# A hybrid decoder layer on one core: where two weight blocks are rounded, which engine makes their low halves, and where the skip factors are scaled

## The chip, the cores and the metric

The kernel runs on one core of one Trainium2 chip. The metric is the device time of one execution, in microseconds (us). Shorter is better. The engines are TensorE (PE: matmuls, with PEld for its weight loads), VectorE (DVE), ScalarE (ACT), GpSimd (POOL) and SyncE (SP, which here only issues DMA transfers). Each engine takes its instructions in the order of its own program.

## The reference, cut to what matters

One layer with 512 tokens of 1024 channels: a normalization, one wide projection, three causal token mixers whose results are gated and added, and a feed-forward part.

```python
h = rms_norm(x, norm1_g[l])
u = h @ w_in[l]                      # 512 x 1024 times 1024 x 11512
(dq, dk, dv, iq, ik, iw, nq, nkv, ng, sz, sxbc, sdt, mg) = jnp.split(u, offsets, axis=-1)
y_a = dsa_mixer(...); y_b = nsa_mixer(...); y_c = ssd_mixer(...)
...
y = y_diag + y_off + xs * d_skip     # in ssd_mixer: d_skip are the skip factors, one for each of 32 heads
...
x = x + mix @ w_out[l]
x = x + jnp.square(jax.nn.relu(rms_norm(x, norm2_g[l]) @ w_ff1[l])) @ w_ff2[l]
```

## The kernel before, in words

**Matmuls in halves.** Every operand of a projection is held as a rounded high half and a low half (the operand minus its high half). `mm3` issues three matmuls for each product: high by high, high by low, low by high. For the activations these halves are `hTh` and `hTl`, for the weights `whi` and `wlo`.

**The start.** x comes in four tiles of 128 tokens (t = 0 to 3). A tile is scaled, turned by eight TensorE transposes into two PSUM buffers `pT` (four transposes each), copied by ScalarE into `hTh` (line 431) and subtracted by VectorE into `hTl` (line 432), once for each half of the tile. There are two `pT` buffers, so the transposes of a tile wait until the `hTl` of the tile before has read them.

**The weight stream.** The class `WS` holds a list of weight blocks of up to 128 x 1024 elements. `load` brings a block into one of three raw buffers (`wraw`) through SP's queue. `split` rounds it on ScalarE (`whi`, line 170) and subtracts on GpSimd or VectorE (`wlo`, line 172); there are six buffers of each half. The set `LOWP` names the blocks whose low half GpSimd makes: block 0 and blocks 4 to 23. Blocks 0 to 3 are the first projection, `c0` (456 columns: keys, values, index parts). Blocks 4 to 11 are the second, `nkv`: 4 to 7 have 512 columns, 8 to 11 have 304. A raw buffer comes free when `wlo` of its block is done.

**The first projection.** `c0` runs tile by tile into two PSUM buffers `pj`. Tiles 0 and 1 fill them; tile 2 can start when the copies of tile 0 (`u0`, lines 682 and 683, and `v_d`, lines 544 and 545) have read its buffer.

**What sets the order.** The program is written as two coroutines, the mixers (`main`) and the projections (`filler`), that take turns by estimated costs. A scheduler then fixes the order on each engine before the run, by priorities and by its own estimate of the times. `tc.issue_after(x)` makes an instruction come after the instruction x in that plan. A small change in one place can so alter the order of many later ones.

**The mixers.** After the start comes the DSA mixer (scores over selected keys), then the state scan of the SSD mixer (16 steps of one group and one chunk, `ssd`, from about 395 us to 556 us), then the NSA mixer, the gated branches and the feed-forward part; projections fill TensorE between the mixers' matmuls. In a scan step, DMA loads `xz` (two buffers), GpSimd makes `xt` and `xw` from it and multiplies it by the skip factors `dskip` (line 1277), and TensorE multiplies `xt` by the decay matrix `E` (line 1303). `ssd_prelude2`, a part of the work between the DSA mixer's units, makes the scan's factors, among them `sv_ea`, and halves `dskip` (line 1226).

Of the kernel before, what the change touches and what calls it, by code (L numbers as in the profile page):

```python
# [9 lines left out]
AF = mybir.ActivationFunctionType  # L10
ALU = mybir.AluOpType
# [12 lines left out]
NS = 6  # L24
RAWB = 3
LEAD = 3
LOWP = {0} | set(range(4, 24))
WE = 2
NH = 4
BH = 2  # L30
# [3 lines left out]
PSB = {"pj": 2, "sc": 2, "pT": 2, "pv": 1, "pF": 1}  # L34
HM = 4000
HP = 3000
WARM = 4, 2
R0, R1, R2, R3 = 1000.0, 1.5, 2.5, 0.5


def build_kernel(ctx, tc, A, out):
    nc = tc.nc
    pe, act, dve, pool = nc.tensor, nc.scalar, nc.vector, nc.gpsimd
# [5 lines left out]
    def bc(ap, shape):  # L49
        return ap.to_broadcast(shape)  # L50

    def f(ap):
        return ap.bitcast(F32)
# [36 lines left out]
    def ps(tag, shape, dt=F32, bufs=2):  # L90
        if tag == XT[0]:
            XT[1] += 1
            if XT[1] % 3 == 0:
                tag = "pF"
        return psp.tile(shape, dt, tag=tag, name=tag, bufs=PSB[tag])
# [9 lines left out]
    hTh = hp_.tile([128, KT, S], F32R, name="hTh")  # L105
    hTl = hp_.tile([128, KT, S], F32R, name="hTl")
# [16 lines left out]
    p = ps("pF", [128, 512])  # L123
# [8 lines left out]
    class WS:  # L132
# [24 lines left out]
        def split(s):  # L157
            i = s.nsplit
            while s.nload <= i:
                s.load()  # L160
            _, n, w = s.specs[i]
            r = s.raw.pop(i)
            m = n * w
            after = None
            if callable(r):
                after = r.after
                r = r(False)
            hi = wp.tile([128, 1024], F32R, name="whi", tag="whi", bufs=NS)
            lo = wp.tile([128, 1024], F32R, name="wlo", tag="wlo", bufs=NS)
            act.activation(hi[:, :m], r[:, :m], AF.Copy)  # L170
            with tc.issue_after(H0[0][1]) if i == 1 else nullcontext():
                (pool if i in LOWP else dve).tensor_tensor(lo[:, :m], r[:, :m], f(hi[:, :m]), op=ALU.subtract)  # L172
            s.hl[i] = (hi[:, :m].rearrange("p (a b) -> p a b", b=w), lo[:, :m].rearrange("p (a b) -> p a b", b=w))
            s.nsplit += 1
            if after is not None:
                after()
# [105 lines left out]
    for q in range(3):  # L282
        m = 0
# [32 lines left out]
    dskip = cp.tile([128, 32], F32, name="dskip")  # L316
# [51 lines left out]
    ss1 = cp.tile([128, NB], F32, name="ss1")  # L368
    rs1 = cp.tile([128, NB], F32, name="rs1")
    H0, XG, g1p = [], [], []  # L370
    wm = ps("pv", [128, 512])

    def warm(n, ref=None):
        with tc.issue_after(getattr(ref, "ins", ref)) if ref is not None else nullcontext():
            for _ in range(n):
                pe.matmul(wm[:, 0:128], ident, ident, start=True, stop=True)
    with tc.high_priority(offset=2 * HP):
        warm(WARM[0])
    ones = x0.tile([128, 128], F32, name="ones")
# [3 lines left out]
    for t in range(NB):  # L383
        with tc.high_priority(offset=0 if t else HP):
            if t == 1:
                with tc.issue_after(H0[0][0]):
                    act.activation(sq_junk, xt[t], AF.Square, accum_out=ss1[:, t:t + 1])
            elif t:
                act.activation(sq_junk, xt[t], AF.Square, accum_out=ss1[:, t:t + 1])
            else:  # L390
                act.activation(sq_junk[:, 0:512], xt[0][:, 0:512], AF.Square, accum_out=ssh[:, 0:1])
                dve.tensor_tensor_reduce(xg, xt[0][:, 512:], xt[0][:, 512:], 1.0, 0.0, ALU.mult, ALU.add, accum_out=ssh[:, 1:2])
                dve.tensor_tensor(ss1[:, 0:1], ssh[:, 0:1], ssh[:, 1:2], op=ALU.add)
                for k0 in range(0, KT, 4):
                    p = ps("pT", [128, 4, 128])
                    for k in range(4):
                        i_ = pe.transpose(p[:, k], xt[t][:, (k0 + k) * 128:(k0 + k + 1) * 128], ident)
                    xg_ = x0.tile([128, 4, 128], F32, name=f"xg{k0}")
                    dve.tensor_tensor(xg_, p, bc(g1c[:, k0:k0 + 4, None], [128, 4, 128]), op=ALU.mult)
                    XG.append(xg_)  # L400
                warm(WARM[1], i_)
            dve.tensor_scalar(ss1[:, t:t + 1], ss1[:, t:t + 1], 1.0 / D, EPS, op0=ALU.mult, op1=ALU.add)
            pool.tensor_tensor(rs1[:, t:t + 1], ss1[:, t:t + 1], mhalf[:, :1], op=ALU.pow)
            if t:
                for i, c in enumerate((0, 512)):
                    dve.scalar_tensor_tensor(xt[t][:, c:c + 512], xt[t][:, c:c + 512], rs1[:, t:t + 1], g1p[i], op0=ALU.mult, op1=ALU.mult)
            else:
                dg = x0.tile([128, 128], F32, name="dg")
                dve.tensor_scalar(dg, ident, rs1[:, 0:1], None, op0=ALU.mult)
                rb = ps("pF", [128, 512])[:, 0:128]  # L410
                i_ = pe.matmul(rb, ones, dg, start=True, stop=True)
                for c in (0, 512):
                    p = ps("sc", [128, 512])
                    with tc.issue_after(getattr(i_, "ins", i_)):
                        pe.matmul(p, one1, g1w[:, c:c + 512], start=True, stop=True)
                    g1p.append(p)
            for k0 in range(0, KT, 4):
                if t:
                    p = ps("pT", [128, 4, 128])
                    for k in range(4):  # L420
                        pe.transpose(p[:, k], xt[t][:, (k0 + k) * 128:(k0 + k + 1) * 128], ident)
                else:
                    hsl = (slice(None), slice(k0, k0 + 4), slice(0, 128))
                    xg_ = XG[k0 // 4]
                    dve.tensor_tensor(xg_, xg_, bc(rb[:, None, :], [128, 4, 128]), op=ALU.mult)
                    h0 = act.activation(hTh[hsl], xg_, AF.Copy)
                    l0 = dve.tensor_tensor(hTl[hsl], xg_, f(hTh[hsl]), op=ALU.subtract)  # L427
                    H0.append([getattr(i, "ins", i) for i in (h0, l0)])
                    continue
                hsl = (slice(None), slice(k0, k0 + 4), slice(t * 128, t * 128 + 128))  # L430
                act.activation(hTh[hsl], p, AF.Copy)
                dve.tensor_tensor(hTl[hsl], p, f(hTh[hsl]), op=ALU.subtract)

    caus = tri("caus", 512, NEG, 0.0, 384, 1, -1)
    vism = tri("vism", 128, NEG, 0.0, -31, 1, 0, [[128, 4], [-16, 32]]).rearrange("p (b n) -> p b n", b=4)
# [2 lines left out]
    for i, b in enumerate((2, 3)):  # L438
        for half in range(2):
            cur = 2 * b + half  # L440
            r = slice(64 * half, 64 * half + 64)
# [770 lines left out]
    def ssd_prelude2(sv, t, tri1, dta):  # L1212
        ones = t["u"]
        pool.memset(ones, 1.0)
        p = ps("pT", [128, 512])
        pe.matmul(p[:, 0:128], tri1, dta, start=True, stop=True)
        pe.matmul(p[:, 128:256], ones, dta, start=True, stop=True)
        dve.tensor_copy(sv["acm"], p[:, 0:128])
        dve.tensor_scalar(sv["nac"], p[:, 0:128], -1.0, None, op0=ALU.mult)
        act.activation(sv["dec"], p[:, 128:256], AF.Exp)  # L1220
        dve.tensor_tensor(t["b"], p[:, 128:256], sv["acm"], op=ALU.subtract)
        act.activation(sv["dw"], t["b"], AF.Exp)
        dve.scalar_tensor_tensor(sv["dw"], sv["dw"], 2.0, sv["dth"], op0=ALU.mult, op1=ALU.mult)
        act.activation(sv["ea"], sv["acm"], AF.Exp)
        dve.tensor_scalar(sv["ea"], sv["ea"], 0.5, None, op0=ALU.mult)
        dve.tensor_scalar(dskip, dskip, 0.5, None, op0=ALU.mult)
        yield 700.0

    def ssd_prelude3(sv, t):
# [438 lines left out]
    def main():  # L1668
        nonlocal at
        HI[0] = 0  # L1670
        yield from dsa_index(mk)
        yield "dq"
        yield "nkv"
        sv, *rest = yield from ssd_prelude()
        at = popen("att", side="right")
        HI[0] = HM
        us = dsa_units()
        us[5].load = lambda: ssd_prelude2(sv, *rest)
        us[7].load = lambda: ssd_prelude3(sv, rest[0])
        yield from pipeline(us, R1)  # L1680
        pclose("att")
        pclose("pre")
        pclose("mask")
        yield from ssd(sv, R3)
        XT[0] = "pT"
        yield "nq"
        at = popen("att", side="right")
        yield from pipeline(nsa_units(R2), R2)
        done.add("nsa")
        yield "c1"  # L1690
        pclose("att")
        pclose("kv")
# [5 lines left out]
    def step():  # L1698
        try:
            v = next(fg)  # L1700
        except StopIteration:
            alive[0] = False
            return None
        return v
# [3 lines left out]
    while True:  # L1708
        with tc.high_priority(offset=HI[0]):
            r = next(mg, None)  # L1710
# [6 lines left out]
        else:  # L1717
            debt += r
            while debt > 0 and alive[0]:
                v = step()  # L1720
# [32 lines left out]
```

## Time and profile before

| what | us |
|---|---|
| median of three timed runs | 1395.9 |
| their range | 1394.72 to 1400.18 |
| the profiled execution, its own time | 1403.27 |
| span of its trace | 1401.5 |
| TensorE busy in that span | 1369.0 |
| VectorE busy | 1001.1 |
| ScalarE busy | 722.0 |
| GpSimd busy | 286.8 |

The profiled execution's own time is 1.8 us above the span of its trace, and 7.4 us above the median of the timed runs, so differences are read from the trace and set on the median. Over the span TensorE was granted 0.986 of its full clock.

### The profile page before, as it was taken

The numbers are of one execution on the slowest core, as the hardware profiler recorded it, in microseconds if no ns is written. First come the engines' busy times: TensorE is split into PE (matmuls) and PEld (weight loads), VectorE is DVE, ScalarE is ACT, GpSimd is POOL, SyncE is SP. The second block draws the span as 40 slices with busy tenths as digits, with TensorE's granted clock in tenths as the row PEclk, the third lists the DMA queues.
The fourth block names the chain that finished last, engine by engine and source line by source line (L and its number), as shares of the span: only waits on it lengthen the run. The fifth ranks groups of instructions, "written<-read, shape, count | busy, mean of one in ns | idle before, by whom it ended". The sixth has DMA issues, their size and how long they took to land.

```text
span 1401.5 us, 19674 instructions
## 1 busy us (share of the span) xinstructions
PE 1369.0 (98%) x6875; PEld 1142.1 (81%) x6875; DVE 1001.1 (71%) x1962; ACT 722.0 (52%) x1434; POOL 286.8 (20%) x235
## 2 busy tenths in 40 slices
PE   8989999999999999999999999999899999999998
PEld 7878888888877778888887888788789888888887
DVE  6499977999877656477667788888635575767841
ACT  5545436667666756366565566555224444444430
POOL 3445211111047375100000002133100201102000
PEclk9999999999999999999999999999999999999999
DMA  6335654644486687735435453435444665746531
GB/s 192 89 96 144 166 179 132 166 113 123 121 259 223 190 257 201 188 100 140 114 114 157 118 146 111 122 117 177 143 150 140 118 177 127 174 116 132 157 117 52
DMA packets 222721, 205.35 MB, mean 147 GB/s; under 512 B 15497, under 2 KB 170013, under 8 KB 222622
## 3 DMA queue, kind: packets, MB, share of 16 engines
q1 hardware_dynamic: 206652, 180.49, 43.7%
q0 software_dynamic: 15232, 20.98, 8.2%
q10 hardware_dynamic: 738, 2.63, 0.6%
q8 instruction: 54, 0.88, 0.3%
q14 instruction: 45, 0.37, 0.1%
HBM read 167.56 MB, written 36.51 MB: 146 GB/s over the span
## 4 chain that ended last, share of the span: by engine, by line
PE 77%; DVE 7%; DMA 7%; issue 4%; POOL 3%; ACT 2%; SPq 0%; DVEq 0%; POOLq 0%; ACTq 0%
PE pj L451 18%; PE pj L453 18%; PE pj L452 18%; PE sc L451 3%; PE sc L452 3%; PE sc L453 3%; DMA gld<-g_d 3%; PE pT L931 2%; PE sc L893 2%; PE sc L892 2%; PE pv L944 2%; DMA wraw<-in_w_in_dram 1%; PE pv L943 1%; POOL mixf L1488 1%; PE sc L1303 1%
## 5 line engine op out<-in xcount | busy, mean ns | idle before, releaser
L170 ACT ACTIVATE whi<-wraw 128x1024 fp32r<-128x1024 f32 (+2 forms) x190 | 198.3, 1048 | 233.8 <-PE pj L452 115.7
L172 DVE TENSOR_TENSOR wlo<-wraw,whi 128x1024 fp32r<-128x1024 f32 (+1 forms) x169 | 215.7, 1280 | 104.5 <-ACT whi L170 102.9
L451 PE MATMUL pj<-hTh,whi 128*128 128x512 f32 x384 | 153.6, 400 | 0.2 <-DVE cacc L824 0.2
L453 PE MATMUL pj<-hTh,wlo 128*128 128x512 f32 x384 | 152.6, 397 | 0.0
L452 PE MATMUL pj<-hTl,whi 128*128 128x512 f32 x384 | 152.3, 397 | 0.0
L451 PE MATMUL pj<-whi,hTh 128*128 128x512 f32 (+2 forms) x352 | 138.7, 394 | 5.9 <-DVE stk L521 3.2
L901 ACT ACTIVATE p<-p,nb,rs 128x256 f32<-128x256 f32 (+3 forms) x192 | 123.2, 645 | 30.6 <-DVE nb L899 30.6
L453 PE MATMUL pj<-whi,hTl 128*128 128x512 f32 (+2 forms) x352 | 137.8, 392 | 0.1
L452 PE MATMUL pj<-wlo,hTh 128*128 128x512 f32 (+2 forms) x352 | 137.6, 391 | 0.0
L451 PE MATMUL pj<-yh,whi 128*128 128x512 f32 (+1 forms) x288 | 109.7, 387 | 11.0 <-DVE gld L1485 6.4
L452 PE MATMUL pj<-yl,whi 128*128 128x512 f32 (+1 forms) x288 | 109.2, 379 | 0.0
L453 PE MATMUL pj<-yh,wlo 128*128 128x512 f32 (+1 forms) x288 | 108.9, 378 | 0.0
L452 PE MATMUL pj<-h2l,whi 128*128 128x512 f32 (+1 forms) x256 | 96.3, 376 | 0.0
L453 PE MATMUL pj<-h2h,wlo 128*128 128x512 f32 (+1 forms) x256 | 96.2, 376 | 0.0
L451 PE MATMUL pj<-h2h,whi 128*128 128x512 f32 (+1 forms) x256 | 96.1, 376 | 0.0
L987 POOL DMA_DIRECT2D qu<-q_d x32 | 23.5, 735 | 334.9 <-PE sc L893 259.3
L451 PEld LDWEIGHTS pj<-hTh,whi 128*128 128x128 f32 x384 | 72.4, 189 | 14.0 <-DVE cacc L824 0.4
L452 PEld LDWEIGHTS pj<-hTl,whi 128*128 128x128 f32 x384 | 72.4, 189 | 13.8 <-issue 0.5
L453 PEld LDWEIGHTS pj<-hTh,wlo 128*128 128x128 f32 x384 | 72.4, 189 | 13.8 <-issue 0.2
L451 PEld LDWEIGHTS pj<-whi,hTh 128*128 128x128 f32 x352 | 67.4, 192 | 19.8 <-issue 5.8
L935 ACT ACTIVATE pth<-pT 128x512 fp32r<-128x512 f32 x95 | 54.5, 592 | 47.4 <-PE pT L931 46.9
L453 PEld LDWEIGHTS pj<-whi,hTl 128*128 128x128 f32 x352 | 67.4, 191 | 12.4 <-DVE hTl L427 0.4
(385 smaller groups left out, 3294.9 us busy)
## 6 DMA issues: line engine op xcount, KB each, us to landing
wraw<-in_w_in_dram SPq DMA_DIRECT2D x84, 512.0 KB, 4.7
wraw<-in_w_ff_dram SPq DMA_DIRECT2D x58, 512.0 KB, 4.3
qd<-in_w_ff_dram POOLq DMA_DIRECT2D x18, 512.0 KB, 6.0
q_d<-qev SPq DMA_DIRECT2D x64, 128.0 KB, 2.5
qu<-q_d POOLq DMA_DIRECT2D x32, 256.0 KB, 3.7
E<-ac_d SPq DMA_DIRECT2D x16, 512.0 KB, 4.9
xz<-xz_d SPq DMA_DIRECT2D x16, 512.0 KB, 5.8
gld<-g_d SPq DMA_DIRECT2D x32, 256.0 KB, 2.8
```

What stands on the lines that cost most here:

```text
L170: act.activation(hi[:, :m], r[:, :m], AF.Copy)
L172: (pool if i in LOWP else dve).tensor_tensor(lo[:, :m], r[:, :m], f(hi[:, :m]), op=ALU.subtract)
L451: pe.matmul(o, lh, rh, start=first, stop=False)
L452: pe.matmul(o, lh, rl, start=False, stop=False)
L453: pe.matmul(o, ll, rh, start=False, stop=last)
L892: pe.matmul(s_[:, h % w, :n], u.q[h], kh[:, :n], start=True, stop=False)
L893: pe.matmul(s_[:, h % w, :n], u.q[h], kl[:, :n], start=False, stop=True)
L901: act.activation(u.p[h][:, :n], u.p[h][:, :n], AF.Exp, bias=u.nb[:, h:h + 1], scale=rs8[:, u.b, u.h0 + h:u.h0 + h + 1], accum_out=u.sm[:, ...
L931: pe.transpose(pt[:, h], u.p[h][:, kb * 128:kb * 128 + 128], ident)
L935: act.activation(ph, ptf, AF.Copy)
L944: pe.matmul(o, vk, pl0, start=False, stop=en)
L987: pool.dma_start(q.rearrange("p (i a) c -> p i (a c)", i=2), src)
```

## The change

Blocks 4 to 7 of the weight stream leave `LOWP`, so VectorE makes their low halves instead of GpSimd. The rounding of block 4 is issued after the copy of the second half of x tile 2 (the third tile) and that of block 5 after the copy of the second half of tile 3 (the fourth): `HX[t]` keeps the last pair of copies of tile t. The halving of the skip factors is issued after the scaling of `sv_ea`. Nothing is computed otherwise.

```diff
-LOWP = {0} | set(range(4, 24))
+LOWP = {0} | set(range(8, 24))
...
+HB = {4: 2, 5: 3}
...
-            act.activation(hi[:, :m], r[:, :m], AF.Copy)
+            with tc.issue_after(HX[HB[i]][0]) if i in HB else nullcontext():
+                act.activation(hi[:, :m], r[:, :m], AF.Copy)
...
+    HX = {}
...
-                act.activation(hTh[hsl], p, AF.Copy)
-                dve.tensor_tensor(hTl[hsl], p, f(hTh[hsl]), op=ALU.subtract)
+                i_ = act.activation(hTh[hsl], p, AF.Copy)
+                l_ = dve.tensor_tensor(hTl[hsl], p, f(hTh[hsl]), op=ALU.subtract)
+                HX[t] = [getattr(v, "ins", v) for v in (i_, l_)]
...
-        dve.tensor_scalar(sv["ea"], sv["ea"], 0.5, None, op0=ALU.mult)
-        dve.tensor_scalar(dskip, dskip, 0.5, None, op0=ALU.mult)
+        i_ = dve.tensor_scalar(sv["ea"], sv["ea"], 0.5, None, op0=ALU.mult)
+        with tc.issue_after(getattr(i_, "ins", i_)):
+            dve.tensor_scalar(dskip, dskip, 0.5, None, op0=ALU.mult)
```

Line numbers behind line 170 are up to five higher in the changed kernel. ScalarE's order at the start, before, from the rounding of block 3 (`whi_350`) on; `whi_362` is block 4, `whi_488` block 5, `pT_236` and `pT_243` are the halves of x tile 2:

```order
L170 ACTIVATE whi_350<-wraw_151 128x912
L170 ACTIVATE whi_362<-wraw_340 128x1024
L1188 ACTIVATE av_1769<-alog_161 128x32
L170 ACTIVATE whi_488<-wraw_342 128x1024
L431 ACTIVATE hTh_103<-pT_236 128x4x128
L431 ACTIVATE hTh_103<-pT_243 128x4x128
```

The same place on ScalarE in the changed kernel, up to block 5; `pT_255` and `pT_262` are the halves of x tile 3:

```order
L434 ACTIVATE hTh_103<-pT_236 128x4x128
L434 ACTIVATE hTh_103<-pT_243 128x4x128
L172 ACTIVATE whi_362<-wraw_340 128x1024
L686 ACTIVATE u0_330<-pj_331 128x64
L687 ACTIVATE u0_330<-pj_331 128x72
L686 ACTIVATE u0_330<-pj_384 128x64
L687 ACTIVATE u0_330<-pj_384 128x72
L434 ACTIVATE hTh_103<-pT_255 128x4x128
L434 ACTIVATE hTh_103<-pT_262 128x4x128
L548 ACTIVATE v_d_316<-pj_331 128x64
L548 ACTIVATE v_d_316<-pj_384 128x64
L172 ACTIVATE whi_488<-wraw_342 128x1024
```

Both roundings moved behind the copies of the x tiles. VectorE's order before, from the low half of block 3 (`wlo_351`) on:

```order
L172 TENSOR_TENSOR wlo_351<-wraw_151,whi_350 128x912
L1226 TENSOR_SCALAR dskip_162<-dskip_162 128x32
L432 TENSOR_TENSOR hTl_104<-pT_236,hTh_103 128x4x128
L432 TENSOR_TENSOR hTl_104<-pT_243,hTh_103 128x4x128
L432 TENSOR_TENSOR hTl_104<-pT_255,hTh_103 128x4x128
L432 TENSOR_TENSOR hTl_104<-pT_262,hTh_103 128x4x128
L545 TENSOR_TENSOR v_d_316<-pj_331,v_d_316 128x64
```

The same place on VectorE in the changed kernel:

```order
L174 TENSOR_TENSOR wlo_351<-wraw_151,whi_350 128x912
L435 TENSOR_TENSOR hTl_104<-pT_236,hTh_103 128x4x128
L435 TENSOR_TENSOR hTl_104<-pT_243,hTh_103 128x4x128
L174 TENSOR_TENSOR wlo_363<-wraw_340,whi_362 128x1024
L435 TENSOR_TENSOR hTl_104<-pT_255,hTh_103 128x4x128
L435 TENSOR_TENSOR hTl_104<-pT_262,hTh_103 128x4x128
L549 TENSOR_TENSOR v_d_316<-pj_331,v_d_316 128x64
```

The halving of `dskip` has left, and the low half of block 4 has come in between the two x tiles. The low halves of blocks 5, 6 and 7 follow later on VectorE, among the small copies of the first projection. TensorE's order is the same in both kernels up to its 1210th matmul.

From the place of the moved `dskip` on, in `ssd_prelude2`, the plan of all engines differs, up to the end of the NSA mixer; the instructions are the same. An example is GpSimd in the third step of the scan, before (`hst` are the states, `xt_4091` and `xw_4093` the third step's products):

```order
L1298 TENSOR_TENSOR hst_4198<-hst_4052,sv_dec_1808 128x512
L1270 TENSOR_TENSOR xt_4091<-xz_4072,sv_dth_1804 128x512
L1273 TENSOR_TENSOR xw_4093<-xz_4072,sv_dw_1806 128x512
L1298 TENSOR_TENSOR hst_4269<-hst_4111,sv_dec_1808 128x512
L1277 TENSOR_TENSOR xz_4072<-xz_4072,dskip_162 128x512
L1265 AFFINE_SELECT E_4135<-E_4135 128x1024
```

The same step in the changed kernel:

```order
L1275 TENSOR_TENSOR xt_4091<-xz_4072,sv_dth_1804 128x512
L1278 TENSOR_TENSOR xw_4093<-xz_4072,sv_dw_1806 128x512
L1303 TENSOR_TENSOR hst_4198<-hst_4052,sv_dec_1808 128x512
L1303 TENSOR_TENSOR hst_4269<-hst_4111,sv_dec_1808 128x512
L1282 TENSOR_TENSOR xz_4072<-xz_4072,dskip_162 128x512
L1270 AFFINE_SELECT E_4135<-E_4135 128x1024
```

One state product has moved behind the two products of `xz`. The number of projection matmuls that TensorE has between two scan steps changes too.

## Rows read from the trace of the kernel before

**Rows 1.** The page's first part: busy us, share of the span, instructions.

```profile
PE 1369.0 (98%) x6875; PEld 1142.1 (81%) x6875; DVE 1001.1 (71%) x1962; ACT 722.0 (52%) x1434; POOL 286.8 (20%) x235
```

**Rows 2.** Waits of TensorE, whole span: us in total, times, longest.

```profile
PE sc L1303 <- POOL xt L1270: 6.3, 4, 2.2
PE pj L451 <- ACT yh L807: 4.6, 2, 2.7
...
PE pj L451 <- DVE v_d L545: 1.6, 1, 1.6
PE pT L421 <- DVE hTl L432: 0.7, 1, 0.7
```

**Rows 3.** Timeline, other engines, 20 to 37 us: start, duration, instruction, [idle before <-releaser].

```profile
20.24 3.00 POOL L172 TENSOR_TENSOR wlo<-wraw,whi 128x1024 fp32r<-128x1024 f32 x1 [3.49 <-ACT whi L170]
...
21.02 2.26 DVE L1226 TENSOR_SCALAR dskip<-dskip 128x32 f32<-128x32 f32 x1
22.37 1.06 ACT L170 ACTIVATE whi<-wraw 128x1024 fp32r<-128x1024 f32 x1 [2.10 <-DMA wraw<-in_w_in_dram]
23.34 1.06 ACT L431 ACTIVATE hTh<-pT 128x512 fp32r<-128x512 f32 x2
...
23.95 1.29 DVE L432 TENSOR_TENSOR hTl<-pT,hTh 128x512 fp32r<-128x512 f32 x2 [0.67 <-ACT hTh L431]
...
25.39 1.20 ACT L431 ACTIVATE hTh<-pT 128x512 fp32r<-128x512 f32 x2 [0.51 <-PE pT L421]
26.02 1.29 DVE L432 TENSOR_TENSOR hTl<-pT,hTh 128x512 fp32r<-128x512 f32 x2 [0.78 <-ACT hTh L431]
...
27.23 0.35 DVE L545 TENSOR_TENSOR v_d<-pj,v_d 128x64 fp32r<-128x64 f32 x2
...
36.24 1.06 ACT L170 ACTIVATE whi<-wraw 128x1024 fp32r<-128x1024 f32 x1 [0.24 <-PE pj L453]
```

**Rows 4.** Timeline of TensorE, 20 to 28 us.

```profile
20.84 1.04 PE L421 MATMUL pT<-ident,x 128*128 128x128 f32 x8
...
24.70 1.26 PE L421 MATMUL pT<-ident,x 128*128 128x128 f32 x8 [0.74 <-DVE hTl L432]
...
27.59 0.45 PE L451 MATMUL pj<-whi,hTh 128*128 128x456 f32 x1 [1.63 <-DVE v_d L545]
```

**Rows 5.** Chain of waits, 20 to 92 us, two links: start, us, what.

```profile
28.77 0.38 PE pj L451
...
31.86 0.20 PE pj L451
```

**Rows 6.** Windows: length, busy us of PE, PEld, DVE, ACT, POOL, granted clock, DMA.

```profile
26.00:28.00 2.00, 0.41 (x2) 0.43 (x3) 1.55 (x4) 1.21 (x4) 0.00 (x0) 0.98 0.58 152
28.00:30.00 2.00, 2.00 (x7) 1.75 (x6) 0.69 (x1) 0.20 (x1) 0.00 (x0) 0.50 0.14 48
```

**Rows 7.** Windows of 50 us, the first two.

```profile
0.00:50.00 50.00, 45.03 (x207) 37.36 (x208) 28.85 (x65) 26.91 (x56) 21.64 (x25) 0.93 0.54 164
50.00:100.00 50.00, 45.73 (x242) 39.14 (x241) 39.03 (x91) 21.54 (x57) 22.04 (x14) 0.97 0.34 95
```

**Rows 8.** The page's groups, low halves on VectorE: busy, mean ns | idle before.

```profile
L172 DVE TENSOR_TENSOR wlo<-wraw,whi 128x1024 fp32r<-128x1024 f32 (+1 forms) x169 | 215.7, 1280 | 104.5 <-ACT whi L170 102.9
```

**Rows 9.** One line's instructions, 1225: ns min/median/max, first and last start.

```profile
L1225 DVE TENSOR_SCALAR sv_ea<-sv_ea x1: 221/221/221, 255.4 to 255.4; 128x128 f32<-128x128 f32 x1
```

**Rows 10.** Timeline of GpSimd, 395 to 440 us, first use of `dskip`.

```profile
401.48 2.01 POOL L1277 TENSOR_TENSOR xz<-xz,dskip 128x512 f32<-128x512 f32 x1
```

**Rows 11.** Timeline of TensorE in the scan, two waits.

```profile
438.79 0.88 PE L1303 MATMUL sc<-xt,E 128*128 128x64 f32 x6 [1.16 <-POOL xt L1270]
463.76 1.44 PE L1303 MATMUL sc<-xt,E 128*128 128x64 f32 x10 [1.77 <-POOL xt L1270]
```

**Rows 12.** Windows of 10 us around them.

```profile
440.00:450.00 10.00, 10.00 (x57) 7.78 (x57) 6.13 (x7) 6.32 (x17) 9.77 (x9) 1.00 0.53 177
460.00:470.00 10.00, 8.23 (x41) 7.08 (x40) 8.03 (x10) 7.77 (x23) 4.57 (x5) 0.83 0.90 284
```

## Prediction

> **What bounds the kernel now.** I read the page first. TensorE is busy for 1369.0 of 1401.5 us [rows 1], so a change gains only where TensorE waits or runs at half clock. The waits of TensorE come next [rows 2]. The start has two of the longer ones: 0.7 us in which the transposes of x tile 3 wait for the `hTl` of tile 2, and 1.6 us in which the first matmul of token tile 2 waits for VectorE's `v_d`. Later the largest are 6.3 us in four waits of the scan for `xt` and 4.6 us in two waits for `yh`.
>
> Then the timeline of the start, on which the reader is to follow one chain [rows 3, 4]. The first eight transposes of x tile 2 run from 20.84 to 21.88. Their copies on ScalarE (`hTh`) start only at 23.34, because block 5's rounding stands ahead in ScalarE's order and waits 2.10 us for its weights, until 22.37, and then takes 1.06. VectorE would not have been ready much earlier: its halving of `dskip`, 128 x 32 elements, began at 21.02 and lasted 2.26 us, until 23.28. That is not its work: GpSimd's low half of block 4 ran from 20.24 to 23.24, and VectorE's instruction ended with it. So one engine held the other off. From there: copies 23.34, low halves 23.95, transposes of tile 3 at 24.70, copies 25.39, low halves 26.02, `v_d` 27.23, TensorE at 27.59.
>
> Last the clock. At 28 us it stood at 0.50 [rows 6]: of the two levels 2.4 GHz was granted before, 1.2 GHz after the wait. A 456-column matmul took 0.38 us there, and 0.20 from about 31.4 on [rows 5]. Ten matmuls started at the slow pace, so the drop cost about 10 x 0.18 = 1.8 us.
>
> **The change, part by part.**
>
> *`dskip` leaves the start.* VectorE gets its 2.26 us back there. At the new place it follows `sv_ea`, which took 0.22 us for four times the elements [rows 9]; 0.22 is its upper bound alone, and 2.26 its bound if GpSimd holds it off again. At either value it costs nothing there if TensorE has projections queued; the first reader of `dskip` stands at 401.48 [rows 10], 146 us later. If that cover were gone, one DSA unit would be late by those 0.2 to 2.3 us.
>
> *Blocks 4 and 5 are rounded later.* ScalarE now takes the copies of tile 2 as soon as they are transposed. Four of the eight transposes are done by about 21.4 (half of 1.04 after 20.84), so the copies can start at about 21.5 instead of 23.34. In before the first copy to the last low half took 23.34 to 25.24, 1.90 us; now that ends at about 23.4. TensorE stopped at 24.70 - 0.74 = 23.96 [rows 4], so the wait of 0.74 us goes. From the transposes of tile 3 to the next matmul the chain is unchanged, 27.59 - 24.70 = 2.89 us, so that matmul starts at 23.96 + 2.89 = 26.85. Gain: **0.74 us**.
>
> What is late next is `v_d` again. The eight transposes now run without a wait, 1.04 us, to 25.00, and TensorE then stands for 26.85 - 25.00 = 1.85 us in one piece, where it stood 0.74 and 1.63. The gain is smaller than the two waits, because the second keeps its chain.
>
> *Their weights.* A raw buffer is held until `wlo` is done. Block 5 was free at about 25.9 and is now free at about 28.5: copies of tile 3, then 1.06 of rounding, then 1.28 of subtraction. SP's loads of blocks 7 and 8 are issued behind these, up to 2.6 us later, and what stands behind them on SP's queue too. ScalarE asks for the next block, block 6, at 36.24, released then by TensorE [rows 3], and for the two after it behind that. A cover of some 8 us hides it; without it TensorE would wait those 2.6 us.
>
> *Four low halves go to VectorE.* 4 x 1.28 = 5.1 us more for VectorE [rows 8], for 3.00 and more each on GpSimd [rows 3]. Block 4's is the only one inside the chain: rounded by about 23.6, subtracted by about 24.9, while the low halves of tile 3 can't start before 23.96 + 1.32 = 25.28 (1.32 is 26.02 less 24.70). So 0.4 us are left. In the first 50 us VectorE is busy for 28.85 [rows 7], so the other three find room. Bounds: nothing, or 1.28 us if the 0.4 don't hold. I take nothing.
>
> A rule of the Trainium skill speaks against this part: "Perfetto Trace Analysis", section "Optimizing Scalar/DVE Operations", says that work may be given away, even to GpSimd, where VectorE is saturated, and warns that the two share a read port. By its first half the move costs up to the 5.1 us of VectorE; by the row of 28.85 it costs nothing; the trace bears out its second half in the 2.26 us of `dskip`.
>
> *The clock.* After the wait of 1.77 us at 463.76 the clock fell, 0.83 in that window; after 1.16 us at 438.79 it stayed at 1.00 [rows 11, 12]. The new stop of 1.85 us is nearer the first. I take the drop as still there: bounds 0 and 1.8 us of gain.
>
> *The plan behind 255 us.* No instruction is added, but the order differs up to the end of the NSA mixer. In that stretch lie the waits for `xt` (6.3) and `yh` (4.6), 10.9 us [rows 2], and behind each of the longer ones a clock drop of about 1.8. In TensorE's order I counted the projection matmuls ahead of the scan's steps. Ahead of the third step there are 13 where there were 16, ahead of the fifth 23 for 16, and ahead of the eighth 23 for 15. Those which waited 1.16 and 1.77 us, the fifth and the eighth [rows 11], have more; the ninth has 6 for 23. At about 0.21 us each (the 0.20 above, for 512 columns) that gives and takes some 1.5 to 3.6 us at a step, in both directions. I take a net of nothing, with bounds of about 8 us on either side.
>
> **Sum.** -0.74 against the profiled execution's own 1403.27 gives 1402.5. That execution lies 7.4 us above the median, so on the median of 1395.9 it is **1395.1 us**. A change under 0.5%, 7 us, can't be told from none on this kernel.
>
> **The rivals.**
>
> *The clock holds at the start.* For it: TensorE's work lies closer together. Against: the drop after 1.77. Then -0.74 - 1.8 = -2.5: 1393.4.
>
> *The new order pays.* The waits of 1.16 and 1.77 go, with one drop of 1.8, and one of the two `yh` waits (2.3 on average): 1.16 + 1.77 + 1.8 + 2.3 = 7.0, with the start's 0.74 7.8 us: 1388.1. For it: 23 for 16 and 23 for 15 matmuls. Against: nothing in the order says that the `yh` waits change.
>
> *The scan runs dry (slower).* Place: the ninth and tenth steps, which have 6 matmuls (for 23) between them and the steps before. The two `xz` buffers tie step nine to the end of step seven: 29 matmuls instead of 38, 1.9 us less cover, and step ten, which waited 2.2 [rows 2], has 36 between the last transposes of `craw` and itself instead of 47, 2.3. With 0.6 at the third step and two more clock drops, 3.6, this is +8.4, less 0.7: 1403.6. It decides from a new stop of about 1.8 us at step nine on, since then the clock falls too.
>
> *VectorE late at the start.* Block 4's subtraction holds up the low halves of tile 3: +1.28 - 0.74, 1396.4. Its margin is the 0.4 us.
>
> *The change does nothing.* Should the copies still wait, 1395.9; the orders shown speak against it.
>
> **How the numbers follow.** Forecast, 0.74 gained and no net from the order: 0.45. Clock holds: 0.10. VectorE late or nothing changed: 0.10. New order pays: 0.20. Scan dry: 0.15. The first three lie within 0.5%: same 0.65, faster 0.20, slower 0.15. The likeliest case alone spans 1391 to 1399; the range of 1387 to 1402.5 takes in most of the fourth, and leaves out the end of the fifth.
>
> **What would show it.** Right: no wait of the transposes at line 421; tile 2's copies at 21.5; the first matmul of token tile 2 at about 26.9; no long `dskip`; clock still 0.50 behind it; at 255 us TensorE 0.7 to 2.5 us ahead. The prediction is wrong if the scan's four waits for `xt` leave 4 to 9 us, or if the sum of TensorE's waits between 255 and 985 us moves by over 5 us either way.

## The result: 0.75% slower, and the profile after

The changed kernel takes **1406.9 us** (median of 5 runs, 1404.69 to 1409.13) where the kernel before takes 1395.9: a ratio of 1.0075 with a 95% interval of 1.0057 to 1.0092. The forecast was 1395.1 us, with a range up to 1402.5 and a chance of 0.15 for slower. It was wrong. Below, the loss is taken as 10.5 us (0.0075 of 1396; the medians differ by 11.0).

The profiled execution of the changed kernel, its first part (busy us, share, instructions):

```profile
PE 1365.7 (97%) x6875; PEld 1135.5 (81%) x6875; DVE 1003.2 (72%) x1966; ACT 720.6 (51%) x1434; POOL 276.2 (20%) x231
```

Its waits of TensorE, the largest four (us in total, times, longest):

```profile
PE pj L455 <- DVE gld L1490: 7.7, 6, 1.8
PE pT L1319 <- DVE yv L1313: 4.7, 3, 2.5
PE pj L455 <- ACT yh L811: 4.6, 5, 1.8
PE sc L1308 <- POOL xt L1275: 4.0, 3, 1.9
```

TensorE is busy for less than in [rows 1], and yet the kernel is slower. The waits for `xt` fell from 6.3 to 4.0 us [rows 2], but 4.7 us for `yv` came in, which before had 0.2. The largest of all, for `gld` of the gated branches, stood in the profile of before too:

```profile
PE pj L451 <- DVE gld L1485: 6.4, 8, 1.9
```

The start of the changed kernel, 20 to 28 us (start, us, instruction, idle before):

```profile
20.40 1.03 PE L424 MATMUL pT<-ident,x 128*128 128x128 f32 x8
21.04 1.09 ACT L434 ACTIVATE hTh<-pT 128x512 fp32r<-128x512 f32 x2 [1.19 <-PE pT L424]
...
22.01 1.06 ACT L172 ACTIVATE whi<-wraw 128x1024 fp32r<-128x1024 f32 x1
...
23.11 1.23 DVE L174 TENSOR_TENSOR wlo<-wraw,whi 128x1024 fp32r<-128x1024 f32 x1
...
23.34 1.03 PE L424 MATMUL pT<-ident,x 128*128 128x128 f32 x8
...
25.82 0.34 DVE L549 TENSOR_TENSOR v_d<-pj,v_d 128x64 fp32r<-128x64 f32 x2
26.17 0.45 PE L455 MATMUL pj<-whi,hTh 128*128 128x456 f32 x1 [1.79 <-DVE v_d L549]
```

It goes as foretold: the copies of tile 2 follow their transposes, the transposes of tile 3 run without a wait, and one stop of 1.79 us (said: 1.85) is left. From the first transposes of tile 2 to this matmul it took 27.59 - 20.84 = 6.75 us [rows 4]; now it is 26.17 - 20.40 = 5.77. But the clock did not fall behind the stop to 0.50, 1.2 GHz, as in [rows 6]; it stayed at 1.00, 2.4 GHz. The windows here (length, busy us of PE, PEld, DVE, ACT, POOL, granted clock, DMA):

```profile
26.00:28.00 2.00, 1.83 (x9) 1.70 (x10) 1.89 (x4) 0.79 (x2) 0.00 (x0) 1.00 0.63 227
28.00:30.00 2.00, 2.00 (x12) 1.81 (x11) 0.10 (x1) 0.00 (x0) 0.00 (x0) 1.00 0.63 161
```

**Two profiles that mislead.** The two spans differ by only 1403.0 - 1401.5 = 1.5 us, the medians by 11. The second profile of the kernel before, taken later (experiment e4_before_again), explains it. Span and granted clock of the first, then of the second profile of before, then of the changed kernel:

```profile
core 0: 1401.5 us, clock 0.986
```

```profile
core 0: 1391.4 us, clock 0.994
```

```profile
core 0: 1403.0 us, clock 0.993
```

A mean clock of 0.986 over 1401.5 us is 19.6 us of TensorE's full-speed work not done, 0.994 over 1391.4 is 8.3, and 0.993 over 1403.0 is 9.8. The first execution thus lost up to 11.3 us more to the clock than the second, with the same program, and its span is 10.1 longer. TensorE's busy time in the second profile agrees:

```profile
PE 1360.0 (98%) x6875; PEld 1133.8 (81%) x6875; DVE 999.1 (72%) x1962; ACT 721.7 (52%) x1434; POOL 288.4 (21%) x235
```

The same matmuls took 1369.0 - 1360.0 = 9.0 us longer in the first, so only 1.1 of the 10.1 us are idle time. Profiled executions are not slow as such: the second one's own time, 1393.2 us, lies at its median of 1393.4. Against the second profile the changed kernel is 11.6 us slower, as by the medians. The loss has to be looked for there.

The clock is not the whole scatter, though. Two executions of e8, with 0.994 and 0.993, took 1401.4 and 1392.8 us. Over the 108 executions of before that were timed beside the experiments, 0.001 less of the clock went with some 0.6 us, where the sum above would make it 1.4.

### The profile page after: what moved, and what is told of

It is laid out like the page before. It is cut to its first block, busy times and chain, and to the rows that moved or that the text cites. A ratio compares the mean times of both kernels' runs of the same rounds, so it can differ in the third digit from the quotient of the medians.

```text
span 1403.0 us, 19683 instructions
## 1 busy us (share of the span) xinstructions
PE 1365.7 (97%) x6875; PEld 1135.5 (81%) x6875; DVE 1003.2 (72%) x1966; ACT 720.6 (51%) x1434; POOL 276.2 (20%) x231
## 4 chain that ended last, share of the span: by engine, by line
PE 76%; DVE 6%; DMA 6%; issue 5%; POOL 4%; ACT 2%; SPq 0%; DVEq 0%; POOLq 0%; ACTq 0%
PE pj L455 18%; PE pj L457 18%; PE pj L456 18%; PE sc L455 3%; PE sc L456 3%; PE sc L457 3%; PE pT L935 2%; DMA gld<-g_d 2%; PE sc L897 2%; DMA E<-ac_d 2%; PE sc L896 2%; PE pv L947 2%; PE pv L948 2%; POOL mixf L1493 1%; DVE wlo L174 1%
```

## The experiments

Each run was timed in 5 rounds beside the kernel before on the same chip. Its medians there were 1394.0 us (e1 to e4), 1393.5 (e5 to e8), 1393.3 (e9 to e12), 1393.7 (e13 to e16) and 1393.0 (e17, e18).

| run | what it has | median us | ratio to before, 95% interval |
|---|---|---|---|
| e1 | edits of the start, `dskip` as before | 1392.8 | 0.9991, 0.9982 to 1.0001 |
| e2 | move of `dskip` alone | 1403.3 | 1.0076, 1.0057 to 1.0094 |
| e3 | whole change, `dskip` at 26 us | 1393.9 | 1.0000, 0.9989 to 1.0011 |
| e4 | the kernel before again | 1393.4 | 0.9992, 0.9981 to 1.0003 |
| e5 | whole change, `dskip` behind `sv_dw` | 1393.4 | 1.0000, 0.9991 to 1.0009 |
| e8 | whole change, `dskip` behind `sv_acm` | 1395.9 | 1.0016, 1.0006 to 1.0027 |
| e12 | whole change, `dskip` behind `sv_dth` | 1392.9 | 0.9994, 0.9985 to 1.0003 |
| e7 | new order up to the end of the scan | 1398.6 | 1.0032, 1.0021 to 1.0044 |
| e6 | new order behind the scan | 1410.7 | 1.0121, 1.0104 to 1.0139 |
| e9 | new order in the scan | 1398.4 | 1.0028, 1.0017 to 1.0039 |
| e10 | new order from the scan to about 900 us | 1399.1 | 1.0032, 1.0020 to 1.0044 |
| e11 | new order from about 900 us on | 1398.3 | 1.0035, 1.0024 to 1.0046 |
| e13 | order of before, as a list | 1393.1 | 1.0001, 0.9990 to 1.0012 |
| e14 | new order in all three stretches | 1404.6 | 1.0083, 1.0066 to 1.0100 |
| e15 | as e14, SyncE's order of before | 1484.5 | 1.0657, 1.0638 to 1.0676 |
| e16 | order of before, GpSimd's new | 1401.5 | 1.0060, 1.0044 to 1.0077 |
| e17 | as e9, GpSimd's order of before | 1413.9 | 1.0142, 1.0123 to 1.0160 |
| e18 | as e14, GpSimd's order of before | 1421.3 | 1.0197, 1.0181 to 1.0213 |

**Which part of the change: e1 to e4.** Against the changed kernel, e1 leaves `dskip` to the scheduler as before, e2 takes the edits of the start back, and e3 puts `dskip` behind the copies of x tile 3. In e1:

```diff
-        with tc.issue_after(getattr(i_, "ins", i_)):
+        with nullcontext():
```

In e2:

```diff
-LOWP = {0} | set(range(8, 24))
+LOWP = {0} | set(range(4, 24))
-HB = {4: 2, 5: 3}
+HB = {}
```

In e3:

```diff
-        with tc.issue_after(getattr(i_, "ins", i_)):
+        with tc.issue_after(HX[3][1]):
```

> The edits of the start alone: blocks 4 to 7 subtracted on VectorE, the roundings of blocks 4 and 5 behind the copies of the x tiles; the halving of dskip stays where it was. TensorE's and SyncE's orders are then those of the kernel before from the first to the last row. Theory A (the new order behind 255 us costs the 11 us): that order is not here, so 0 to 3 us faster than before, 1393 to 1396, and with no low half on GpSimd beside it the halving of dskip is short, under 0.5 us for the 2.26 of before. Theory B (the edits of the start cost it, through weights that come late behind VectorE's low halves): 1404 to 1409.

> The move of dskip alone; the start is that of before. TensorE's and SyncE's orders are those of the changed kernel from the first to the last row. Theory A: the new order is here, so 8 to 14 us slower than before, 1404 to 1410, at least as slow as the changed kernel. Theory B: the start is as before, so within 3 us of before.

> The whole change, but the halving of dskip is issued after the last low half of x tile 3 and not after the scaling of sv_ea: it leaves its old place, and TensorE's and SyncE's orders are those of before in every row. Theory A: 0 to 4 us faster than before, 1392 to 1396. Theory B: 1404 to 1409, as the changed kernel.

> The kernel before once more, unchanged, for a second profile, since the first lay 7.4 us above the median of its own timed runs, and for the scatter of a comparison in which nothing differs. Both theories: 1395 to 1398 and a ratio of 1.000 within 0.2 per cent. If the profile is again 5 us or more above the median, profiled executions are slow as such; if it lies near the median, the first one was a chance.

Theory A holds and B falls: the move of `dskip` alone makes the whole loss (1.0076 against 1.0075; its 1403.3 us lie just under the 1404 to 1410 expected), and the edits of the start cost nothing. They also gain nothing that can be told from the scatter of e4. The row of `dskip` in e1 (ns min/median/max, first and last start):

```profile
L1231 DVE TENSOR_SCALAR dskip<-dskip x1: 181/181/181, 21.1 to 21.1; 128x32 f32<-128x32 f32 x1
```

Where it took 2.26 us beside GpSimd's low half [rows 3], it takes 0.18 at the same place without one. But that meeting was one execution's. The start of the kernel before in its second profile:

```profile
18.91 2.40 POOL L172 TENSOR_TENSOR wlo<-wraw,whi 128x1024 fp32r<-128x1024 f32 x1 [2.48 <-ACT whi L170]
...
22.20 0.17 DVE L1226 TENSOR_SCALAR dskip<-dskip 128x32 f32<-128x32 f32 x1
...
27.33 0.44 PE L451 MATMUL pj<-whi,hTh 128*128 128x456 f32 x1 [1.80 <-DVE v_d L545]
```

Here GpSimd is done at 18.91 + 2.40 = 21.31, `dskip` takes 0.17 us, and no transpose waits for `hTl`. The wait of 0.74 us that the change takes away was not in every execution. From the first transposes of tile 2, at 21.36, to the matmul at 27.33 it took 5.97 us, so against this profile the changed kernel's 5.77 gain 0.20.

**The instruction or the plan: e5, e8, e12.** `dskip` is halved at three other places of the work in and ahead of `ssd_prelude2`. All three edits are of this kind:

```diff
-        dve.scalar_tensor_tensor(sv["dw"], sv["dw"], 2.0, sv["dth"], op0=ALU.mult, op1=ALU.mult)
+        i_ = dve.scalar_tensor_tensor(sv["dw"], sv["dw"], 2.0, sv["dth"], op0=ALU.mult, op1=ALU.mult)
+        with tc.issue_after(getattr(i_, "ins", i_)):
+            dve.tensor_scalar(dskip, dskip, 0.5, None, op0=ALU.mult)
...
-        with tc.issue_after(getattr(i_, "ins", i_)):
-            dve.tensor_scalar(dskip, dskip, 0.5, None, op0=ALU.mult)
```

> The whole change, but the halving of dskip stands behind the scaling of sv_dw, a few VectorE instructions ahead of where the change puts it. There the scheduler plans every other instruction as it does with dskip early: TensorE's, SyncE's and GpSimd's orders are those of before behind the start, VectorE's too but for dskip itself. Theory A1 (the order behind 255 us costs the 10 us, the instruction itself nothing): within 3 us of before, 1391 to 1397. Theory A2 (a VectorE instruction at some 253 us costs it, by what it delays there): 1401 to 1407.

> The whole change, but the halving of dskip stands behind the copy of sv_acm, some ten VectorE instructions ahead of where the change puts it. The scheduler then makes a third plan: TensorE's order differs from both kernels' in 2114 and 3086 places. It is a draw of another order by a cause that has nothing to do with what the order is good for. Theory P1 (any other plan loses, since the plan of before is a lucky one among many): 1399 to 1407. Theory P2 (the changed kernel's plan is an unlucky one, others are like before's): 1391 to 1397. Theory A2: as the changed kernel, 1401 to 1407.

> The whole change, but the halving of dskip stands behind the scaling of sv_dth, at about 230 us: a fourth plan, 2357 of TensorE's places away from before's and 3310 from the changed kernel's. Theory P1 (before's plan is the lucky one): 3 to 11 us slower than before. Theory P2 (the changed kernel's is an unlucky one): within 3 us of before, as with the halving behind sv_acm, which was 2.2 us slower.

In e5 the instruction runs where the change wanted it, and costs nothing. Its row there, then that of the changed kernel:

```profile
L1229 DVE TENSOR_SCALAR dskip<-dskip x1: 166/166/166, 255.1 to 255.1; 128x32 f32<-128x32 f32 x1
```

```profile
L1231 DVE TENSOR_SCALAR dskip<-dskip x1: 179/179/179, 252.6 to 252.6; 128x32 f32<-128x32 f32 x1
```

TensorE's sequence of matmuls in e5's trace is that of before from the first to the last. So the place of the instruction costs nothing: A1 holds and A2 falls. The other half, that the order costs it without the instruction at that place, is shown by e14 below (`dskip` at 26 us, new order, 0.83%). Of four plans, before's and e12's are equally fast, e8's costs 2.2 us, and the changed kernel's 10.5. Theory P1, that any other plan loses, falls.

**Where: e6, e7, e9 to e11, e13, e14.** The orders are written out as a list for all engines, and each instruction is tied behind the one ahead of it on its engine:

```diff
+def impose(nc, tc):
+    """Issue every engine's instructions in the order PLAN (places in the program's order)."""
...
+        i = traced[at]
+        if i.engine in last:
+            tc.add_manual_dep(i, last[i.engine].name,
+                              mybir.DependencyInfo(mybir.DependencyClass.NoSync, mybir.DependencyReason.DATA),
+                              reason="plan")
+        last[i.engine] = i
...
             build_kernel(ctx, tc, aps, out)
+            impose(nc, tc)
```

> The whole change but for dskip, which stands at the start; every engine's order is written out as a list: that of the kernel before up to the end of the scan (the first transposes of rst), and from there what is left in the changed kernel's order. The part behind the scan is so tried alone. Theory S (most of the loss lies in the scan, where VectorE's yv and GpSimd's xt come later for TensorE): 0 to 3 us slower than before, 1393 to 1397. Theory G (most of it lies behind the scan, in the waits for yh and gld of the gated branches): 6 to 11 us slower, 1399 to 1405. By the waits in the two profiles it would be about 2.5 us of waits, 1396 to 1399, between the two.

> The changed kernel, with every engine's order written out as a list: its own up to the end of the scan (the first transposes of rst), and from there what is left in the order of the kernel before. 57 instructions, 32 projection matmuls among them, which before stand ahead of that place, come right behind it. Theory S: 6 to 11 us slower than before, 1399 to 1405. Theory G: 0 to 3 us slower, 1393 to 1397. By the waits in the two profiles it would be about 4 us of waits, 1397 to 1400. If the two halves add up, what this one and the one before it cost together is the 9 to 11 us of the whole.

> The start as in the changed kernel with dskip early; every engine's order is written out as a list: that of before, but between two places of the program at which both plans have issued the same instructions to within three (ahead of the scan, about 388 us, and behind it, about 575 us) that of the changed kernel. By the times at which two profiles of either order reach these places the new order takes 1.5 to 6 us longer between them. Theory M (each stretch costs by its own waits, and the parts add up): 1.5 to 5 us slower than before. Theory S (the scan alone): 8 to 11 us slower. Theory G (nothing in the scan): within 1 us of before.

> As the run with the new order in the scan, but the changed kernel's order stands between the place behind the scan (about 575 us) and one in the last part of the NSA mixer (about 900 us) at which both plans have issued exactly the same instructions. By the profiles the new order takes about 4.5 us longer between them. Theory M: 3 to 5 us slower than before. Theory S: within 1 us. Theory G, with the loss at the gated branches' last waits: within 1 us.

> As the run with the new order in the scan, but the changed kernel's order stands from the place in the NSA mixer at about 900 us on; from about 965 us on the two orders are one again. By the profiles the new order takes about 3.4 us longer up to there and 1.7 us longer behind it. Theory M: 3 to 5 us slower than before. Theory S: within 1 us. Theory G: 8 to 11 us slower. If M holds, the three parts together make 9 to 11 us.

> The start as in the changed kernel with dskip early, and the order of the kernel before, written out as a list for every engine: a control. If the list by itself costs nothing: within 1.5 us of before. If it costs what the three stretches have too much together (13 us for 10.5): about 1 us slower.

> As the runs with the new order in one stretch, but in all three, from about 388 us to the end. Theory M (the parts add up): 9 to 13 us slower than before, 1402 to 1407. If the stretches hide one another's losses: below 8 us.

Neither S nor G, but M: each stretch costs, 0.28%, 0.32% and 0.35%, in sum 0.95% where all three at once (e14) cost 0.83% and the change 0.75%. Within the intervals the parts add up, and a list by itself costs nothing (e13). e7, the scan and what is ahead of it, costs 4.5 us, and e9 shows that the scan's order makes up nearly all of that. e6 can't be used for a share: at its seam, at 571 us, TensorE stood for 5.2 us, where every other run has at most 0.9 us of this kind. Likely it had by then spent the projections that the new order keeps for later; the profile names no releaser ("issue"), so this is not shown:

```profile
PE sc L1032 <- issue: 5.2, 1, 5.2
```

What the stretches lose is read from e2, which has the old start, against the second profile of before. The windows start and end where both orders have issued the same matmuls (at 575 us, to within three). Windows of before (second profile) and of e2 (columns as above):

```profile
388.43:575.05 186.62, 179.16 (x937) 143.23 (x935) 118.23 (x141) 116.74 (x302) 111.83 (x87) 0.98 0.76 230
575.05:899.72 324.67, 321.11 (x1659) 269.58 (x1658) 246.36 (x645) 193.72 (x408) 21.98 (x20) 1.00 0.44 128
899.72:1042.11 142.39, 135.17 (x725) 114.32 (x724) 98.81 (x213) 61.26 (x129) 27.86 (x18) 1.00 0.46 146
```

```profile
387.86:576.78 188.92, 178.29 (x937) 141.61 (x935) 122.94 (x153) 115.88 (x302) 109.55 (x87) 0.99 0.75 229
576.78:906.06 329.28, 324.99 (x1660) 270.31 (x1658) 244.87 (x641) 193.76 (x411) 23.89 (x20) 0.99 0.44 126
906.06:1052.43 146.37, 137.15 (x724) 115.42 (x723) 97.47 (x206) 60.74 (x127) 26.96 (x18) 0.99 0.46 142
```

The stretches are 2.3, 4.6 and 4.0 us longer, 10.9 in sum, with as many matmuls in each. TensorE's waits in them, before (second profile), one stretch after the other:

```profile
PE sc L1303 <- POOL xt L1270: 5.5, 4, 2.2
...
PE pT L1314 <- DVE yv L1308: 0.3, 1, 0.3
...
PE pj L451 <- ACT yh L807: 1.9, 2, 1.6
...
PE pj L451 <- DVE gld L1485: 7.2, 9, 1.7
```

And in e2:

```profile
PE pT L1319 <- DVE yv L1313: 4.4, 3, 2.9
PE sc L1308 <- POOL xt L1275: 4.1, 4, 1.9
...
PE pj L455 <- ACT yh L811: 3.9, 4, 2.0
...
PE pj L455 <- DVE gld L1490: 7.9, 9, 2.2
PE pj L456 <- DVE yl L812: 1.2, 1, 1.2
```

In the scan `yv` costs 4.1 us more and `xt` 1.4 less; behind it `yh` costs 2.0 more, and in the last stretch `yl` and `gld` 1.9 more. Of these, `yv`, `xt` and `yl` differ alike in both profiles of either order. `yh` does not: before had 4.6 us of it in its first profile [rows 2] and 1.9 in its second, so the 2.0 can be chance.

TensorE's idle time in the three windows is 653.68 - 635.44 = 18.24 us before and 664.57 - 640.43 = 24.14 in e2: of 10.9 us, 5.9 are idle time. The other 5.0 are longer busy time. The missing clock, added up over windows of 5 us, is 3.4 us before and 5.1 in e2, which explains 1.7 of them; what the other 3.3 are stays open. Most of this lies in the middle stretch, where idle time grows by only 0.7 of its 4.6 us: that the new order costs there is shown (e10), but not by what.

The longest of the new waits, in the scan of e2:

```profile
431.70 1.67 PE L1308 MATMUL sc<-xt,E 128*128 128x64 f32 x14
...
433.05 1.50 DVE L832 SCALAR_TENSOR_TENSOR craw<-cth,cacc 128x512 f32<-128x512 f32 x1
434.07 1.59 POOL L1294 TENSOR_TENSOR t<-t,xz 128x512 f32<-128x512 f32 x1
434.46 1.75 DVE L1313 TENSOR_TENSOR yv<-yv,xz 128x512 f32<-128x512 f32 x1
...
436.26 0.65 PE L1319 MATMUL pT<-ident,yv 128*128 128x128 f32 x4 [2.89 <-DVE yv L1313]
```

The like place of the kernel before, second profile:

```profile
426.13 1.48 DVE L828 SCALAR_TENSOR_TENSOR craw<-cth,cacc 128x512 f32<-128x512 f32 x1
427.14 1.59 POOL L1289 TENSOR_TENSOR t<-t,xz 128x512 f32<-128x512 f32 x1
427.16 1.90 PE L1303 MATMUL sc<-xt,E 128*128 128x64 f32 x16
427.54 1.75 DVE L1308 TENSOR_TENSOR yv<-yv,xz 128x512 f32<-128x512 f32 x1
...
429.35 0.66 PE L1314 MATMUL pT<-ident,yv 128*128 128x128 f32 x4 [0.29 <-DVE yv L1308]
```

VectorE does the same in both, `craw` and then a `yv` of 1.75 us beside GpSimd's `t`. Before, TensorE has sixteen matmuls of the next step in that time. In the new order its fourteen are over at 433.4 and nothing stands between them and the transposes of `yv`. Not a slower instruction makes the wait, but what TensorE has to do meanwhile.

**Which engine's order: e15 to e18.** The lists mix two orders: that of SyncE or GpSimd from one plan, the rest from the other. The orders of TensorE, VectorE and ScalarE were not taken from different plans, so no run says what each of them is worth.

> As the run with the new order in all three stretches, but SyncE issues its transfers in the order of the kernel before (190 of 536 places differ). Theory D (transfers issued later behind others on SyncE's queue make the new order slow): within 3 us of before. Theory N (the order of TensorE, VectorE and ScalarE does it, the queue's follows from it): 9 to 13 us slower, or more, since the queue then fits neither.

> The order of the kernel before on all engines but GpSimd, which has the changed kernel's from the scan on (38 of 246 places differ, most of them in the scan, where its products of xz come ahead of a state product). Theory X (GpSimd's order makes xt and yv late in the scan): 2 to 5 us slower, as the run with the new order in the scan. Theory N: within 1.5 us of before.

> As the run with the new order in the scan, which was 3.9 us slower than before, but GpSimd keeps the order of before. Theory X (GpSimd's order is what loses in the scan): within 1.5 us of before. Theory N (the others' order loses, GpSimd's fits it): 4 us or more.

> As the run with the new order in all three stretches, which was 11 us slower than before, but GpSimd keeps the order of before. Theory X: 5 to 8 us slower, the shares of the two later stretches alone. Theory N: 11 us or more.

D and X both fall, and N is right for all but e16, where it expected nothing. Either mix is slower than both plans: GpSimd's new order under the old ones costs 0.60%, more than the new scan as a whole (0.28%), and its old order under the new ones makes the kernel with the new scan 1.42% slower than before, and that with all three stretches 1.97%, where e14 lost 0.83%. The scan's waits for GpSimd in e17:

```profile
PE sc L1308 <- POOL xt L1275: 11.5, 4, 7.5
PE pT L1361 <- POOL rst L1359: 6.1, 1, 6.1
```

With SyncE's old order (e15) TensorE waits in the scan for `xt` and for transfers of `bcx`:

```profile
PE sc L1308 <- POOL xt L1275: 18.4, 3, 15.8
PE pv L1269 <- DMA bcx<-bct_d: 15.6, 4, 6.1
```

Neither of these two engines' orders can be exchanged alone: the orders are a set, and a mix does not tell what share of the loss is whose.

## Why the prediction was wrong

- **"`dskip` leaves the start ... at either value it costs nothing there."** Right for the instruction (0.17 to 0.18 us at 253 to 255 us, e5 at 1.0000).
- **"Gain: 0.74 us."** Right in its chain: no wait at the transposes, one stop of 1.79 us. The copies started 0.64 us behind the first transposes (said: 0.66), and of the 0.4 us of margin ahead of tile 3's low halves 0.28 were left. Its size can't be seen in the medians (e1 1.2 us faster, e3 and e5 nothing, e4 0.6 with no change at all), and the second profile of before shows why it is not always there to be gained: against it the chain gained 0.20 us.
- **"Their weights" and "four low halves"**: hidden, as said; e3 and e5 have both edits and lose nothing. The rule cited from the Trainium skill, "Perfetto Trace Analysis", section "Optimizing Scalar/DVE Operations", has two halves. The trace agrees with its warning that the two engines can hold each other up, by `dskip` at 2.26 and 0.18 us and by `yv` beside GpSimd's product, 1.75 us; that a port is the cause no run shows. Its advice for a saturated VectorE did not apply: VectorE was busy for little more than half of that time [rows 7].
- **"I take the drop as still there."** Not so in the profile after; see the last section.
- **"I take a net of nothing, with bounds of about 8 us on either side."** This step failed. The new order costs 10.5 us by itself (e2, 7.9 to 13.1; 9.3 by its medians), above the bound, and in e14, with 9.2 to 13.9, clear of it. They were made from projection matmuls counted ahead of scan steps and from two waits, and so left out the stretches behind the scan, which hold two of three shares (e10, e11), and the wait for `yv`, the largest in the new scan. The waits for `xt` and `yh` were not the largest of before, as the prediction has it: `gld` had 6.4 us in eight. And a sum of waits leaves out the longer busy time, some half of the loss. (The 0.21 us for a matmul of 512 columns is low, too: 0.20 x 512 / 456 is 0.22, which makes the largest step 3.8 us for 3.6.)
- **"The prediction is wrong if ..."** Neither sign was clear. The waits for `xt` were left with 4.0 us, at the edge of 4 to 9, and the sum of TensorE's waits between 255 and 985 us went from 13.1 to 17.2 us between the first profiles, by 4.1 and not over 5. Signs made of waits alone did not show a loss of 10.5 us.
- **The rival that the scan runs dry** had the right sign and nearly the time (1403.6), by the wrong place. The scan costs about 4 us (e9) and not 8.4, and not through `xt`, whose waits fell. That it came near is luck; and the range, up to 1402.5, left out this rival's own figure, to which the prediction gave 0.15.
- **"A change under 0.5% ... can't be told from none."** It can be here: e9, e10 and e11, at 0.28 to 0.35%, have intervals clear of 1.
- **The base.** That differences are set on the median and not on the first profile was right: its span lies 10.1 us above the second's.

No version tried is faster than before beyond the uncertainty. If the edits of the start are kept, then as in e1, e3 or e5, which leave the plan behind the start as it was and cost nothing.

## What to carry to other kernels

Where a scheduler plans the whole program, a move of one 0.2 us instruction is a change of everything behind it: compare the planned orders first, and where they differ, look for a place (e3, e5) at which they don't. Two other new plans (e12, e8) gave 0 and 2.2 us, this one 10.5, so the spread over re-plans belongs in the range, over every stretch with waits and not the one that is easiest to count. Before two profiles are subtracted, multiply each span by its missing clock (a rough bound on what the clock cost), and take a second profile of the reference. A wait that differs between two profiles of one program, as `yh` does here, explains nothing in a third.

## What the runs showed of the hardware

**A clock drop is no fixed property of a stop.** The kernel before, same program, stop of 1.80 us at 27.33, second profile:

```profile
28.00:30.00 2.00, 2.00 (x11) 1.81 (x11) 0.67 (x1) 0.00 (x0) 0.00 (x0) 1.00 0.03 8
```

In its first profile the clock stood at 0.50 there [rows 6], after 1.63 us; in e2, which has the same start, it stayed at 1.00 after 1.64. Of the 17 profiled executions with the new start, 7 show a drop to about 0.5 behind the stop, and 10 none: none of the six with a stop of 1.79 or 1.80 us, and seven of the eleven with 1.88. So the length of the stop alone does not decide it here. A drop can be priced only as a chance, here about 1.8 us in two of five.

**Of two products that overlapped, the later one was stretched.** `yv` took 1.75 us where a GpSimd product of 1.59 began 0.4 us ahead of it, and its shortest in e2 was 0.68 us. It ended 0.55 us after GpSimd's in both rows above. Where `yv` began first, it took its 0.69 us, and GpSimd's product grew: `xt`, 1.04 us at the median, took 1.53 in the second profile of before, and TensorE then waited 1.76 us for it.

```profile
459.74 0.69 DVE L1308 TENSOR_TENSOR yv<-yv,xz 128x512 f32<-128x512 f32 x1
459.79 1.53 POOL L1270 TENSOR_TENSOR xt<-xz,sv_dth 128x512 f32<-128x512 f32 x1 [3.42 <-DMA xz<-xz_d]
```
